# Elementwise arithmetic moved from GpSimd to VectorE in a float32 encoder of an S5 layer and a spatial-gating layer

## The chip, the core and the metric

The kernel runs on one core of a Trainium2 chip. The metric is device time in microseconds (us) of one execution, as the median of several runs. The profiled execution is a separate one, of which the hardware profiler recorded every instruction.

## The reference, cut to what matters

Two layers over 256 tokens of 2048 channels, all in float32. Each layer has a token mixer and a feed-forward part; each of these four parts ends with an RMSNorm of its sum, whose weights multiply it before it is added to the residual stream, and the next part begins with another RMSNorm.

```python
for i in range(DEPTH):                       # 2 layers
    g = norm_g[i]
    hn = rms_norm(h, g[0])
    m = s5_mixer(hn, ...) if i % 2 == 0 else sgu_mixer(hn, ...)
    h = h + rms_norm(m, g[1])
    f = squared_relu_mlp(rms_norm(h, g[2]), ffn_w_up[i], ffn_w_down[i])
    h = h + rms_norm(f, g[3])
```

`rms_norm(x, g)` is `x * rsqrt(mean(x * x) + eps) * g`. The S5 mixer ends with a gated linear unit: `z = gelu(y); z = z * sigmoid(z @ w_glu); return z @ w_out`, where `y` comes from a linear recurrence over time.

## The kernel before

The 256 tokens are two token tiles of 128 (`n` is 0 or 1). Every large product is split into three to keep float32 accuracy: a weight `w` is sent as a high half `hi` (rounded to the matrix engine's fast format, made by ScalarE in line 145) and a low half `lo = w - hi` (line 146, on the engine in `state["lo"]`), and the activations likewise; a step multiplies hi by hi, hi by lo and lo by hi (lines 166 to 172).

A **panel** is 1024 output columns; a **step** of a panel is 128 rows of weights, so twelve products of 512 columns (three products, two column halves, two token tiles). Weights come in chunks of two steps, on the DMA queue of SP, into three buffers, from the gated linear unit on four; a chunk's buffer is free, and the next chunk's load is issued, when the low half of its last step is made (lines 148 to 152). `issue_cast` (lines 133 to 152) makes high and low halves two steps ahead of the products; `state["hold"]` stops it, and `force` overrides that. There are three buffers each for high and low halves. Smaller work is put between steps with `at(delay, fn)`, which runs `fn` so many steps later. The order of the instructions on each engine is the order in which the program writes them out; nothing reorders them.

The order of work around the change:

- **The end of a part** is `Tail.run` (lines 354 to 407). Its first panel (output columns 0 to 1023) is evicted by `take`, squared for the norm's sum, and multiplied by the norm's weights on GpSimd (`scaled(G, 0, n)`, line 360). The second panel runs all but its last three steps for both token tiles; then the three steps are run for tile 0 alone (line 374), then for tile 1, half by half (lines 384 and 386). Behind tile 0's products VectorE evicts them, works out the norm's factor (`rstd`: fifteen small operations, among them line 334 and three Newton steps in lines 246 to 248) and makes the residual of block 0 of tile 0 (`resid`, line 351; a block is 512 columns).
- The next part begins with `next_panel` (lines 409 to 464): TensorE transposes block 0 of tile 0 (`tiles(0)`, line 298, which reads the residual), ScalarE and VectorE make high and low halves of it (lines 305 and 307), and TensorE runs three steps for tile 0. Meanwhile VectorE makes the factor and the residual of tile 1, and TensorE does the same for tile 1. Blocks 1 to 3 follow between later steps (`hook`). The first two low halves of weights of the next part are made on GpSimd (`state["lo"] = G` in line 389 and the forced `issue_cast` in line 390), and so are the products of the second panel with the norm's weights (line 453).
- There are three such **seams**: S5 mixer to feed-forward, feed-forward to spatial gating, and spatial gating to the second feed-forward. The fourth tail has `dst` and ends the kernel: there two residuals of tile 0 go through ScalarE and GpSimd (`resid_g`, lines 343 to 347), and the output is stored by SP (`put`).
- In the **gated linear unit's first panel** (lines 1047 to 1083) all low halves up to step 12 are made on GpSimd (lines 1047 and 1082). Between its steps stand the last part of the recurrence: `scan_some(3, 99)` in line 1066, forty operations on VectorE over the last 512 channels, written behind step 2; `y_group` on TensorE, with ScalarE's copies; and `z_t`, transposes of `z`.

## Time and profile before

| | us |
|---|---|
| median of 3 runs | 2763.17 |
| lowest and highest run | 2760.88, 2763.52 |
| span of the profiled execution | 2762.2 |
| TensorE busy in it (products) | 2678.5 |
| VectorE busy | 1598.9 |
| ScalarE busy | 1260.0 |
| GpSimd busy | 102.6 |

TensorE is busy for 97% of the span, VectorE for 58%, ScalarE for 46% and GpSimd for 4%. The granted TensorE clock is 0.979 of full speed on the mean. Times in the trace are counted from the start of the span. In a row, the numbers in front are the start and the duration in us, the name of the engine follows (PE is TensorE, DVE VectorE, ACT ScalarE, POOL GpSimd, SPq the issuing queue of SP), then the line of the kernel, the operation, the tiles written and read, their shapes and the number of instructions that the row merges. In square brackets stands how long the engine was idle just before, and what it waited for. A pair of merged rows on one engine can overlap a little, as instructions are pipelined.

### The profile page before, as it was taken

Reading aid. Unit: us, or ns where it says so; the run is one execution under the profiler, and the core shown is the slowest. Engines: PE = TensorE matmul, PEld = TensorE weight load, DVE = VectorE, ACT = ScalarE, POOL = GpSimd, SP = SyncE. Lnnn points to the kernel's source line nnn. Section 1 sums busy time; section 2 is a strip of 40 time slices with the busy share of each in tenths; the row PEclk is TensorE's granted clock in tenths of the full one; section 3 lists DMA queues with packets and bytes.
Section 4 is the critical chain, followed back from the end, with each engine's and each line's share of the span. In section 5 each row is a group of like instructions: output and inputs, shape, how many; then the busy total and the mean of one; then the engine's idle time right before and its main releaser. Section 6 shows DMA issues by size and latency. Waiting matters only on the chain.

```text
span 2762.2 us, 30556 instructions
## 1 busy us (share of the span) xinstructions
PE 2678.5 (97%) x12327; PEld 2159.4 (78%) x12327; DVE 1598.9 (58%) x1798; ACT 1260.0 (46%) x1440; POOL 102.6 (4%) x60
## 2 busy tenths in 40 slices
PE   8989998999999999989999999999989999999997
PEld 4547887888888888778887788888868888888885
DVE  6684456545555555675547745555575455555556
ACT  5455544544443444454444544444444444444443
POOL 0103101000000000110000000000010000000001
PEclk9987999999999999999999999999999999999998
DMA  7432574555555555565656555555645555555553
GB/s 185 139 107 73 173 231 164 190 190 185 193 186 196 185 188 192 183 185 197 198 191 204 184 198 183 192 189 193 220 167 186 195 188 193 184 197 184 193 187 107
DMA packets 149437, 502.29 MB, mean 182 GB/s; under 512 B 21792, under 2 KB 30128, under 8 KB 147888
## 3 DMA queue, kind: packets, MB, share of 16 engines
q1 hardware_dynamic: 148704, 500.02, 53.8%
q8 instruction: 96, 1.57, 0.2%
q10 hardware_dynamic: 592, 0.33, 0.0%
q14 instruction: 45, 0.37, 0.0%
HBM read 494.02 MB, written 6.29 MB: 181 GB/s over the span
## 4 chain that ended last, share of the span: by engine, by line
PE 90%; DVE 3%; ACT 2%; issue 2%; POOL 0%; DVEq 0%; POOLq 0%; ACTq 0%
PE acc L171 82%; PE acc L183 2%; PE tr L264 2%; PE acc L892 1%; PE tr L1237 1%; PE acc L895 1%; DVE lo L146 0%; PE acc L827 0%; DVE st L246 0%; DVE st L247 0%; DVE st L248 0%; ACT g L881 0%; DVE g L351 0%; POOL lo L146 0%; ACT hi L145 0%
## 5 line engine op out<-in xcount | busy, mean ns | idle before, releaser
L171 PE MATMUL acc<-hi,sl_g 128*128 128x512 f32 x6912 | 1886.0, 392 | 2.5 <-DVE g L321 1.1
L171 PEld LDWEIGHTS acc<-hi,sl_g 128*128 128x128 f32 x6912 | 1298.1, 189 | 276.6 <-ACT sl_g L305 2.7
L146 DVE TENSOR_TENSOR lo<-raw,hi 128x1024 fp32r<-128x1024 f32 x639 | 791.6, 1241 | 654.5 <-ACT hi L145 647.3
L171 PE MATMUL acc<-lo,sl_g 128*128 128x512 f32 x3456 | 1067.9, 390 | 3.3 <-DVE lo L146 2.6
L145 ACT ACTIVATE hi<-raw 128x1024 fp32r<-128x1024 f32 x652 | 691.0, 1061 | 797.4 <-PE acc L171 794.9
L171 PEld LDWEIGHTS acc<-lo,sl_g 128*128 128x128 f32 x3456 | 649.5, 188 | 140.6 <-DVE lo L146 3.7
L146 DVE TENSOR_TENSOR lo<-spare,hi 128x1024 fp32r<-128x1024 f32 x206 | 252.5, 1226 | 287.0 <-ACT hi L145 287.0
L145 ACT ACTIVATE hi<-spare 128x1024 fp32r<-128x1024 f32 x212 | 224.7, 1061 | 324.7 <-PE acc L171 324.7
L269 DVE TENSOR_TENSOR sl_g<-tr,sl_g 128x512 fp32r<-128x512 f32 x104 | 67.3, 687 | 115.1 <-ACT sl_g L268 115.1
L340 POOL TENSOR_TENSOR g<-g,big 128x1024 f32<-128x1024 f32 x16 | 41.9, 2631 | 2302.8 <-ACT big L329 2294.9
L183 PE MATMUL acc<-raw,g 128*128 128x512 f32 x256 | 122.6, 626 | 0.1
L268 ACT ACTIVATE sl_g<-tr 128x512 fp32r<-128x512 f32 x104 | 57.1, 595 | 87.8 <-PE tr L264 87.4
L183 PEld LDWEIGHTS acc<-raw,g 128*128 128x128 f32 x256 | 49.2, 201 | 53.4 <-issue 52.5
L1144 DVE TENSOR_TENSOR g<-acc,g 128x1024 f32<-128x1024 f32 x48 | 56.4, 1217 | 0.0
L264 PE MATMUL tr<-ident,big 128*128 128x128 f32 x416 | 55.9, 276 | 0.1
L264 PEld LDWEIGHTS tr<-ident,big 128*128 128x128 f32 x416 | 48.9, 142 | 8.4 <-ACT big L1238 1.7
L892 PE MATMUL acc<-big,g 128*64 128x64 f32 x256 | 36.2, 281 | 10.7 <-issue 6.3
L901 ACT ACTIVATE big<-acc 32x256 f32<-32x256 f32 x64 | 23.9, 374 | 40.9 <-PE acc L895 40.2
L1123 DVE TENSOR_TENSOR big<-big 128x1024 f32<-128x1024 f32 x32 | 39.2, 1226 | 5.2 <-ACT big L1122 3.0
L892 PEld LDWEIGHTS acc<-big,g 128*64 128x64 f32 x256 | 25.8, 176 | 19.7 <-issue 8.9
L1122 ACT ACTIVATE big<-acc,st 128x1024 f32<-128x1024 f32 x32 | 35.8, 1119 | 8.7 <-PE acc L171 8.7
L1238 ACT ACTIVATE big<-tr,bsT 128x384 f32<-128x384 f32 x32 | 18.6, 582 | 41.7 <-PE tr L1237 40.7
(174 smaller groups left out, 927.8 us busy)
## 6 DMA issues: line engine op xcount, KB each, us to landing
raw<-in_ffn_w_up_dram SPq DMA_DIRECT2D x96, 1024.0 KB, 5.0
raw<-in_ffn_w_down_dram SPq DMA_DIRECT2D x96, 1024.0 KB, 5.3
raw<-in_sgu_w_in_dram SPq DMA_DIRECT2D x72, 1024.0 KB, 5.0
raw<-in_sgu_w_out_dram SPq DMA_DIRECT2D x36, 1024.0 KB, 5.3
spare<-in_ffn_w_up_dram SPq DMA_DIRECT2D x32, 1024.0 KB, 5.0
spare<-in_ffn_w_down_dram SPq DMA_DIRECT2D x32, 1024.0 KB, 5.3
spare<-in_sgu_w_in_dram SPq DMA_DIRECT2D x24, 1024.0 KB, 5.1
raw<-in_s_w_in_dram SPq DMA_DIRECT2D x15, 1024.0 KB, 6.1
```

The costliest lines, as they stand in the source:

```text
L145: S.activation(out=hi, in_=src, func=AF.Copy)
L146: state["lo"].tensor_tensor(out=lo, in0=src, in1=hi.bitcast(F32), op=ALU.subtract)
L171: T.matmul(half(ps, j), lhsT=l, rhs=r[:, j * 512:(j + 1) * 512], start=first and w == 0, stop=last and w == which[-1])
L183: T.matmul(ps[n][:, j * 512:(j + 1) * 512], lhsT=lhs[n], rhs=raw_t[i][:, k, j * 512:(j + 1) * 512], start=first, stop=last)
L264: T.transpose(out=ps[:, a * 256 + n * 128:a * 256 + n * 128 + 128], in_=src(kt + a, n), identity=ident)
L268: S.activation(out=slab.hi[:, o:o + 512], in_=ps, func=AF.Copy)
L269: V.tensor_tensor(out=slab.lo[:, o:o + 512], in0=ps, in1=slab.hi32[:, o:o + 512], op=ALU.subtract)
L340: eng.tensor_tensor(out=self.m[:, n, c], in0=self.m[:, n, c], in1=self.gbc[:, c], op=ALU.mult)
L892: T.matmul(o[gp], lhsT=dst[:, q, gp, :], rhs=w2[:, 2 * r + gp, :], start=True, stop=False)
L1122: S.activation(out=tmp[n], in_=ps[n], func=AF.Relu, scale=rs[:, n:n + 1])
L1123: V.tensor_tensor(out=tmp[n], in0=tmp[n], in1=tmp[n], op=ALU.mult)
L1144: V.tensor_tensor(out=acc[:, n, c], in0=ps[n], in1=acc[:, n, c], op=ALU.add)
```

## The change

All elementwise arithmetic of GpSimd goes to VectorE, and some of it to another place in the order:

- `state["lo"]` is gone: every low half is made on VectorE, in the tails, in the gated linear unit and elsewhere.
- `scaled(0, n)` is put behind steps 2 and 4 of the tail's second panel.
- `scaled(1, 0)` stands right behind the first residual of tile 0 in `run`; `scaled(1, 1)` stands in `next_panel` behind the transposes of block 1.
- The forced casts of the next part's first two steps at the end of `run` are gone; `issue_cast(first + 3, True)` in `next_panel`, which stays, now makes all of the first three, behind the copies of `tiles(0)`.
- The last tail has its own order: tile 1's first half is run before tile 0's factor is worked out, `resid_g` is gone, and residuals are made 1024 columns at a time, each followed by its stores.

```diff
-        def scaled(self, eng, p, n):
+        def scaled(self, p, n):
             c = slice(p * 1024, (p + 1) * 1024)
-            eng.tensor_tensor(out=self.m[:, n, c], in0=self.m[:, n, c], in1=self.gbc[:, c],
-                              op=ALU.mult)
-
-        def resid_g(self, b, n):
-            c = slice(b * 512, (b + 1) * 512)
-            S.activation(out=self.m[:, n, c], in_=self.m[:, n, c], func=AF.Copy, scale=self.r[n])
-            G.tensor_tensor(out=self.h[:, n, c], in0=self.h[:, n, c], in1=self.m[:, n, c],
-                            op=ALU.add)
-
-        def resid(self, b, n):
-            c = slice(b * 512, (b + 1) * 512)
+            V.tensor_tensor(out=self.m[:, n, c], in0=self.m[:, n, c], in1=self.gbc[:, c],
+                            op=ALU.mult)
+
+        def resid(self, b, n, nb=1):
+            c = slice(b * 512, (b + nb) * 512)
             V.scalar_tensor_tensor(out=self.h[:, n, c], in0=self.m[:, n, c], scalar=self.r[n],
                                    in1=self.h[:, n, c], op0=ALU.mult, op1=ALU.add)
...
             for n in range(2):
-                self.scaled(G, 0, n)
+                at(2 + 2 * n, lambda n=n: self.scaled(0, n))
...
             if dst is not None:
-                self.scaled(G, 1, 0)
+                split_steps(*args, 1, [((0,), all3)])
+                srcs = [self.take(ps, 1, 1, 0)]
+                self.square(srcs[0], 1, 1)
+                self.rstd(0)
+                self.scaled(1, 0)
+                split_steps(*args, 1, [((1,), all3)])
+                for b in (0, 2):
+                    self.resid(b, 0, 2)
+                    put(0, b, b + 2)
+                srcs.append(self.take(ps, 1, 1, 1))
+                self.square(srcs[1], 2, 1)
+                split_done(panels[1], nk - 3, nk)
+                self.scaled(1, 1)
+                self.rstd(1)
+                for b in (0, 2):
+                    self.resid(b, 1, 2)
+                    put(1, b, b + 2)
+                return
             self.rstd(0)
-            if dst is None:
-                self.resid(0, 0)
-            else:
-                self.resid_g(2, 0)
+            self.resid(0, 0)
+            self.scaled(1, 0)
             split_steps(*args, 1, [((0,), all3)])
             srcs = [self.take(ps, 1, 1, 0)]
             split_steps(*args, 1, [((1,), all3)])
             srcs.append(self.take(ps, 1, 1, 1))
             split_done(panels[1], nk - 3, nk)
-            state["hold"], state["lo"] = False, G
-            issue_cast(panels[1][0] + nk + 2, True)
+            state["hold"] = False
...
-            state["lo"] = V
             tiles(0)
             issue_cast(first + 3, True)
             self.last()
             self.rstd(1)
             self.resid(0, 1)
-            for n in range(2):
-                self.scaled(G, 1, n)
...
             issue_cast(first + 5, True)
             trans(1)
+            self.scaled(1, 1)
             run_panel(panel, slabs, ps, 3, hook=hook)
...
         y_group(0, 2)
-        state["lo"] = G
         issue_cast(glu_p[0][0] + 2, True)
...
         z_t(1, 3)
-        state["lo"] = V
         run_panel(glu_p[0], slab_z, pg, 11, 16)
```

## Rows read from the trace of the kernel before

**Rows 1.** The chain of work that ended last: its line by engine on the page, with shares of the span, and one piece of the chain in order of time (start, us, what).

```profile
PE 90%; DVE 3%; ACT 2%; issue 2%; POOL 0%; DVEq 0%; POOLq 0%; ACTq 0%
...
914.74 84.35 PE acc L171 x372
```

**Rows 2.** TensorE's waits over the whole span, the longest in total (engine, line waited for, us in total, times, longest).

```profile
PE tr L298 <- DVE g L351: 28.2, 6, 8.4
```

**Rows 3.** GpSimd's groups of instructions by line and shape (count, busy us and mean ns, idle time before them and what ended it).

```profile
L340 POOL TENSOR_TENSOR g<-g,big 128x1024 f32<-128x1024 f32 x16 | 41.9, 2631 | 2302.8 <-ACT big L329 2294.9 <-issue 5.2 <-DVE g L325 2.7
...
L146 POOL TENSOR_TENSOR lo<-raw,hi 128x1024 fp32r<-128x1024 f32 x13 | 31.3, 2419 | 65.1 <-ACT hi L145 65.1
```

**Rows 4.** The timeline of the second seam, all engines, in order of start.

```profile
1170.22 0.16 DVE L334 SCALAR_TENSOR_TENSOR st<-st 128x1 f32<-128x1 f32 x1 [0.41 <-ACT big L329]
...
1171.90 4.64 POOL L146 TENSOR_TENSOR lo<-spare,hi 128x1024 fp32r<-128x1024 f32 x2 [14.53 <-ACT hi L145]
...
1171.95 2.30 DVE L246 TENSOR_TENSOR st<-st 128x1 f32<-128x1 f32 x1
...
1179.63 1.28 DVE L321 TENSOR_TENSOR g<-acc,g 128x512 f32<-128x512 f32 x2
...
1179.77 1.11 PE L298 MATMUL tr<-ident,g 128*128 128x128 f32 x4 [7.74 <-DVE g L351]
...
1180.49 1.15 ACT L305 ACTIVATE sl_g<-tr,gT 128x128 fp32r<-128x128 f32 x4 [7.78 <-PE tr L298]
...
1181.15 1.13 DVE L307 SCALAR_TENSOR_TENSOR sl_g<-tr,gT,sl_g 128x128 fp32r<-128x128 f32 x4 [0.24 <-ACT sl_g L305]
...
1184.21 2.21 DVE L334 SCALAR_TENSOR_TENSOR st<-st 128x1 f32<-128x1 f32 x1
...
1190.36 0.73 PE L171 MATMUL acc<-hi,sl_g 128*128 128x512 f32 x2 [0.24 <-ACT sl_g L305]
```

**Rows 5.** Two prices on VectorE: the product of two 128x1024 tiles (group by line, over the whole span), and two low halves of weights in a row (timeline, from 1236).

```profile
L1123 DVE TENSOR_TENSOR big<-big 128x1024 f32<-128x1024 f32 x32 | 39.2, 1226 | 5.2 <-ACT big L1122 3.0
...
1236.05 2.34 DVE L146 TENSOR_TENSOR lo<-raw,hi 128x1024 fp32r<-128x1024 f32 x2
```

**Rows 6.** The timeline of the first seam, VectorE, and TensorE's first product for the second token tile.

```profile
443.03 0.16 DVE L334 SCALAR_TENSOR_TENSOR st<-st 128x1 f32<-128x1 f32 x1 [0.50 <-ACT big L329]
...
457.13 0.14 DVE L253 TENSOR_TENSOR st<-st 128x1 f32<-128x1 f32 x1
...
457.58 0.16 DVE L334 SCALAR_TENSOR_TENSOR st<-st 128x1 f32<-128x1 f32 x1
...
459.98 0.75 DVE L351 SCALAR_TENSOR_TENSOR g<-g,st,g 128x512 f32<-128x512 f32 x1
...
461.68 0.73 PE L171 MATMUL acc<-hi,sl_g 128*128 128x512 f32 x2 [0.24 <-ACT sl_g L305]
```

**Rows 7.** The timeline: a wait of TensorE in the first seam's last panel, and its first transposes in the third seam.

```profile
408.94 0.74 PE L171 MATMUL acc<-lo,sl_g 128*128 128x512 f32 x2 [0.34 <-DVE lo L146]
...
2022.02 1.11 PE L298 MATMUL tr<-ident,g 128*128 128x128 f32 x4 [7.68 <-DVE g L351]
```

**Rows 8.** The timeline of the gated linear unit's first panel: the scan on VectorE (its first and last operation, one plain one of 480 elements, and the three longest), the high half of the fifth step on ScalarE, and on TensorE the sixth step's first products and the transposes behind the eighth.

```profile
241.55 1.19 DVE L856 TENSOR_TENSOR g<-g,sc_t 128x992 f32<-128x992 f32 x1 [0.63 <-ACT g L838]
...
245.96 1.06 ACT L145 ACTIVATE hi<-raw 128x1024 fp32r<-128x1024 f32 x1
...
246.20 0.66 DVE L856 TENSOR_TENSOR g<-g,sc_t 128x480 f32<-128x480 f32 x1
...
247.34 2.80 DVE L858 TENSOR_TENSOR g<-g,g 128x480 f32<-128x480 f32 x1
...
256.57 2.47 DVE L859 TENSOR_TENSOR g<-g,g 128x224 f32<-128x224 f32 x1
...
259.08 2.72 DVE L856 TENSOR_TENSOR g<-g,sc_t 128x480 f32<-128x480 f32 x1
...
265.47 0.71 PE L171 MATMUL acc<-hi,sl_g 128*128 128x512 f32 x2
...
267.09 1.19 DVE L859 TENSOR_TENSOR g<-g,g 128x992 f32<-128x992 f32 x1
...
274.75 0.60 PE L264 MATMUL tr<-ident,big 128*128 128x128 f32 x4
```

**Rows 9.** Busy time by stretch: the stretch and its length; then busy us and instructions of PE, PEld, DVE, ACT and POOL; then the granted clock, the DMA share and GB/s.

```profile
240.00:252.00 12.00, 8.22 (x65) 6.35 (x65) 11.18 (x14) 6.91 (x7) 2.54 (x1) 0.64 0.24 89
...
275.00:296.00 21.00, 20.64 (x179) 16.16 (x178) 3.26 (x5) 14.08 (x25) 6.71 (x3) 1.00 0.53 183
...
1180.00:1186.00 6.00, 5.97 (x17) 4.46 (x17) 5.28 (x10) 3.42 (x9) 1.98 (x1) 0.55 1.17 232
```

**Rows 10.** The timeline of TensorE behind its wait in the spatial gating layer.

```profile
1463.72 0.73 PE L171 MATMUL acc<-lo,sl_g 128*128 128x512 f32 x2 [2.27 <-DVE lo L146]
...
1465.21 1.00 PE L171 MATMUL acc<-lo,sl_g 128*128 128x512 f32 x2
...
1468.77 0.92 PE L171 MATMUL acc<-hi,sl_g 128*128 128x512 f32 x2
```

**Rows 11.** The timeline of the end of the kernel: VectorE's eviction of the first token tile, and SP's first stores of the last eight.

```profile
2738.95 1.29 DVE L321 TENSOR_TENSOR g<-acc,g 128x512 f32<-128x512 f32 x2 [1.76 <-PE acc L171]
...
2755.66 1.72 SPq L368 DMA_DIRECT2D out_dram<-g  x4
```

More of the change, by code (lines that the diff above doesn't have):

```diff
@@ L94 @@
     chunks, steps = [], []
-    state = {"dma": 0, "done": 0, "cast": 0, "step": 0, "ext": None, "lo": V, "hold": True}
+    state = {"dma": 0, "done": 0, "cast": 0, "step": 0, "ext": None, "hold": True}
     raw_t, hi_t, lo_t = {}, {}, {}
@@ L145, in issue_cast @@
                 S.activation(out=hi, in_=src, func=AF.Copy)
[L146 removed]
+                V.tensor_tensor(out=lo, in0=src, in1=hi.bitcast(F32), op=ALU.subtract)
                 hi_t[s], lo_t[s] = hi, lo
@@ L395, in run @@
             self.last = last
-            if dst is not None:
-                self.last()
-                for b in range(2):
-                    self.resid(b, 0)
-                self.resid_g(3, 0)
-                self.scaled(G, 1, 1)
-                self.rstd(1)
-                put(0)
-                for b in range(4):
-                    self.resid(b, 1)
-                    if b % 2:
-                        put(1, b - 1, b + 1)
         def next_panel(self, panel, slabs, gcol):
```

1 line of the change is left out of this document (removed).

## Prediction

> **What bounds the kernel now.** I read the chain that ended last first [rows 1]: TensorE carries 90% of it, so a change on other engines is worth only what it does to TensorE's waits. The list of those waits comes second [rows 2]: its largest entry is the transposes of line 298 waiting for VectorE's line 351, 28.2 us in six waits. These six are the three seams between layers, two at each: at the end of a layer TensorE has nothing to multiply until the residual of the first 512 columns is done, once for each token tile. Third, what GpSimd does [rows 3]: 16 products with the norm's weights at 2631 ns and 19 low halves at some 2.4 us, at the seams and in one other place, the gated linear unit's first panel.
>
> The timeline of the second seam shows why VectorE is late there [rows 4]. Its Newton steps are 128x1 operations. The one at 1171.95 takes 2.30 us and ends at 1174.25; GpSimd's pair of low halves starts at 1171.90 and has 2.32 us for each, so its first ends at 1174.22. The operation of line 334 has the same size and takes 0.16 us at 1170.22, with GpSimd silent, and 2.21 us at 1184.21, with GpSimd at work. The reader should see that VectorE's small operations last as long as GpSimd's large ones beside them, and that TensorE waits 7.74 us behind this.
>
> **The change at the three seams.** Removed there: two low halves and two products on GpSimd. Added to VectorE: the product `scaled(1, 0)` between the first residual and the evictions, two more low halves, and `scaled(1, 1)` after the second block's transposes. I work out VectorE's new line, in program order, for the second seam. Line 334 starts at 1170.22, as before. From line 334 to the residual takes 2.40 us where GpSimd is silent (457.58 to 459.98 [rows 6]), so the first residual starts at 1172.62. Behind it on VectorE: that residual 0.75 [rows 6], product 1.23 [rows 5], two evictions 1.28 and four low halves of transposed blocks 1.13 [rows 4], three low halves of weights at 1.17, 3.5 [rows 5], the second rstd 2.85 (457.13 to 459.98 [rows 6]): 10.74 us. So the second token tile's residual starts at 1183.36. From there to its first product takes 1.70 us (459.98 to 461.68 [rows 6]): 1185.06 against 1190.36 [rows 4], **5.3 us gained**. ScalarE does not break the line: four copies are 1.15 us [rows 4] and a high half is 1.06 [rows 8], and both run under the product and the evictions.
>
> First seam, same sum: 443.03 + 2.40 + 10.74 + 1.70 = 457.87 against 461.68 [rows 6], **3.8 us**; it is less since GpSimd's last product stretched nothing there. Third seam: its first wait is 7.68 us [rows 7] against 7.74, so 5.3 us again. Together **14.4 us**. In the first seam's last panel TensorE also waited 0.34 us for a low half that GpSimd's products had delayed [rows 7]; I take these **0.3 us**.
>
> What is late next: TensorE still waits, first about a microsecond for the first residual, then some 2 us for the first high half (ScalarE now makes all three behind the copies), then about 3 us for the second residual, because two low halves and a product stand before it. The products `scaled(0, n)` stand behind two steps of the last panel. A step is twelve products at 0.227 us (84.35 us for 372 [rows 1]), 2.7 us, and holds one low half of 1.2, so they are covered; without that cover each costs its 1.23. `scaled(1, 1)` is covered likewise, with the low halves of two steps ahead of it. The weight load that the first two casts release moves back on SP by some 3 us, and behind the loads that the next layer issues; several chunks are in flight, so I count zero, and a microsecond at each seam if they are not enough.
>
> **The gated linear unit.** Thirteen low halves go back to VectorE, whose scan of the last 512 channels ran beside GpSimd's. In program order the fifth low half stands before the scan, the sixth and seventh behind it. The fifth's high half is made at 245.96 and takes 1.06 us, ScalarE being full until then [rows 8]. VectorE began the scan at 241.55; now it first waits for 247.02 and makes the low half, 1.2 us, so the scan starts at 248.3. In return its stretched operations shrink: 2.80, 2.47 and 2.72 us where such a one takes 0.66 or less [rows 8], 6.0 us in all. Its length, 241.55 to 268.28, falls from 26.7 to 20.7; it ends at 269.0, and the sixth low half is there at 270.2. TensorE reached that step at 265.47 and will stand behind two products, some 4 us. After 270.2 it has ten products and two steps, 7.7 us, to reach 277.9, where it was at 274.75 before [rows 8]: **3.1 us lost**. The bounds are 0 and 4.2, all that the wait can be.
>
> **The clock.** From 1180 to 1186, right behind the 7.74 us wait, the granted clock is 0.55, near the lower of its two levels [rows 9]; that is in the numbers above, and goes or stays with the wait. Behind one wait of 2.27 us two products took 0.73 us at 1463.72, but 1.00 at 1465.21 and still 0.92 at 1468.77; by an estimate half of these 3.5 us, 1.7, was lost [rows 10]. The new waits, 3 us at each seam and 4 us in the linear unit, lie between these. Bounds: 0 to 1.7 at each seam; 0 to 6.8 in the linear unit (half speed over some 13.6 us, as around 250, where the clock is 0.64 [rows 9]). I take **1.0** for each seam: the 2.27 us row is the nearest, but I do not expect all three to pay it; and **2.0** in the linear unit, by the same row and a longer wait.
>
> **The end of the kernel.** The last stage is VectorE, ScalarE and GpSimd alone. New: the second token tile's first half is evicted at about 2741.7 (2738.95 [rows 11], nine products, half of 1.28), then rstd 2.85, product 1.23, two wide residuals at most 1.5 each (twice 0.75), eviction 0.64, square 1.06 at most (as a high half of twice its width [rows 8]), product 1.23, rstd 2.85, wide residual 1.5: 2756.0 at most. Before, the first of the last eight stores was issued at 2755.66 [rows 11], and SP's issue of these eight sets the end. What the stretched operations give back is paid for by the products in line. I count 0, and half a microsecond either way.
>
> **Sum:** -14.4 - 0.3 + 3.0 (clock, seams) + 3.1 + 2.0 (linear unit) = -6.6 us. The profiled span is 2762.2; the median of the runs is 2763.17, 1.0 above. From the median: **2756.6 us**.
>
> **Rivals.** (a) *The linear unit costs nothing*, because TensorE comes later to the sixth low half than before: without the 5.1 us the time is 2751.5. Against it: TensorE's waits ahead of it are on ScalarE, and stay. 0.17, with what lies between. (b) *The clock eats it*: 1.7 at each seam and 6.8 in the linear unit: -14.7 + 5.1 + 3.1 + 6.8 = 0.3, or 2763.5. For it: every long wait in the trace has a slow stretch behind it; against it: whole panel steps come behind the new ones, not sparse work. 0.25 for the space from 2757.6 to there. (c) *Slower*: the stretching is not GpSimd's doing but belongs to small operations beside ScalarE's casts. Then the first residual comes as before, and the 3.5 us of added work (product and two low halves) less the 2.1 us of line 334 stand in the line: 1.4 us later at each seam, 3.5 if line 334 stays long; with 5.1 in the linear unit 2772 to 2779. It decides as soon as one Newton step still shows over 2 us. Against it: the coinciding ends. 0.04. (d) *VectorE becomes the bound of the linear unit's panel*, with all thirteen low halves paid, 16.0 us in place of 3.1: 2769.5. For it: VectorE is busy 11.18 of 12 us from 240 to 252; against it: 3.26 of 21 from 275 to 296 [rows 9], so the work has room on either side of the scan. 0.04. The Trainium skill, page Perfetto Trace Analysis, section Optimizing Scalar/DVE Operations, gives this rule: when VectorE is saturated, moving some work to another engine, even GpSimd, may make sense. It adds that these two share a read port, so that it might not help; the trace bears the first half out for the scan alone, and the second at the seams. That the change does not do what it says I exclude, by the diff.
>
> **How the numbers follow.** The forecast, 2753.5 to 2757.6, has 0.50; (a) 0.17, (b) 0.25, (c) and (d) 0.08. A measurement of this kernel can tell about 0.2%, 5.5 us, from no change; that border is 2757.6. So faster 0.67, same 0.25, slower 0.08. The range runs from below (a) to near (b), 2750 to 2762.5; it leaves out (c), (d) and the ends.
>
> **What would show it.** No arithmetic is left on GpSimd; all 128x1 operations take near 0.16 us; line 298's waits fall from 28.2 to some 13 us; line 171 waits for line 146 near 266, about 4 us; the granted clock behind each seam's second wait shows which of the two clock cases holds. I am wrong if Newton steps stay long, if the clock falls at every seam and for long in the linear unit, or if the scan starts near 241 as before.

## The result, and the profile after

The changed kernel took 2744.64 us (median of 5 runs, 2743.36 to 2752.01), the kernel before 2760.88 us in the same comparison (5 runs, 2756.96 to 2763.52). The ratio is 0.9947, with a 95% interval of 0.9932 to 0.9963. That is 16.2 us less, where 6.6 were forecast. Three of all executions in this document, whose granted clock was 0.45 to 0.71 on the mean, took 3586 us or more and are left out of every median and range.

The first line of the page: GpSimd is left with 12.8 us, all of it memsets and set-up. VectorE is busy for no longer than before (1598.9 us then), although it does GpSimd's work as well.

```profile
PE 2670.4 (97%) x12327; PEld 2154.8 (79%) x12327; DVE 1591.8 (58%) x1831; ACT 1258.2 (46%) x1438; POOL 12.8 (0%) x23
```

TensorE's waits over the whole span (engine, line waited for, us in total, times, longest). The first entry is what [rows 2] show as 28.2 us; the other two are new or grown: TensorE now waits once for a low half in the linear unit (4.1 us), and at each seam for the first high half (2.0).

```profile
PE tr L298 <- DVE g L345: 6.7, 6, 2.0
...
PE acc L171 <- DVE lo L146: 6.3, 2, 4.1
PE acc L171 <- ACT hi L145: 5.9, 3, 2.0
```

The second seam's timeline, which answers to [rows 4]. Look at three things. No small operation is long: line 334 has 0.16 us, and so have all others. TensorE's first transposes wait 1.32 us where they waited 7.74. The second wait is 0.53 us, because the twelve products ahead of it take 5.49 us, where the same twelve take 3.09 at full clock (`scan_split`, shown further down).

```profile
1162.33 0.16 DVE L334 SCALAR_TENSOR_TENSOR st<-st 128x1 f32<-128x1 f32 x1 [0.41 <-ACT big L329]
...
1164.65 0.75 DVE L345 SCALAR_TENSOR_TENSOR g<-g,st,g 128x512 f32<-128x512 f32 x1
1165.32 1.22 DVE L340 TENSOR_TENSOR g<-g,big 128x1024 f32<-128x1024 f32 x1
1165.46 0.66 PE L298 MATMUL tr<-ident,g 128*128 128x128 f32 x4 [1.32 <-DVE g L345]
...
1168.07 5.49 PE L171 MATMUL acc<-hi,sl_g 128*128 128x512 f32 x12 [1.96 <-ACT hi L145]
...
1174.86 0.75 DVE L345 SCALAR_TENSOR_TENSOR g<-g,st,g 128x512 f32<-128x512 f32 x1
1175.67 0.66 PE L298 MATMUL tr<-ident,g 128*128 128x128 f32 x4 [0.53 <-DVE g L345]
...
1176.56 0.72 PE L171 MATMUL acc<-hi,sl_g 128*128 128x512 f32 x2 [0.24 <-ACT sl_g L305]
```

Busy time by stretch (stretch, length, busy us of PE, PEld, DVE, ACT, POOL, then the granted clock). The half clock lies ahead of 1176, between the two waits; behind the second wait it is 1.00.

```profile
1166.00:1172.00 6.00, 4.04 (x11) 3.13 (x10) 6.00 (x10) 5.24 (x11) 0.00 (x0) 0.59 0.44 67
1172.00:1176.00 4.00, 3.47 (x13) 2.44 (x12) 3.08 (x17) 0.00 (x0) 0.00 (x0) 0.77 0.78 264
1176.00:1182.00 6.00, 5.76 (x31) 4.68 (x30) 4.90 (x8) 3.84 (x8) 0.00 (x0) 1.00 0.10 11
```

The 0.55 of [rows 9] belongs to the same place in the kernel before: between its two waits, on the same twelve products. Behind its second wait, of 2.11 us, the clock was 1.00 too. Its timeline of TensorE, and the stretch behind that wait:

```profile
1180.91 5.08 PE L171 MATMUL acc<-hi,sl_g 128*128 128x512 f32 x12
...
1189.46 0.66 PE L298 MATMUL tr<-ident,g 128*128 128x128 f32 x4 [2.11 <-DVE g L351]
```

```profile
1189.40:1195.40 6.00, 5.70 (x31) 4.67 (x31) 4.51 (x9) 3.45 (x7) 0.00 (x0) 1.00 0.00 0
```

The linear unit's first panel, which answers to [rows 8]: VectorE waits for the fifth high half, makes the low half, and only then begins the scan; the operation that took 2.80 us takes 0.65; the sixth low half stands behind the whole scan, and TensorE behind it.

```profile
239.97 1.23 DVE L146 TENSOR_TENSOR lo<-raw,hi 128x1024 fp32r<-128x1024 f32 x1 [6.51 <-ACT hi L145]
241.11 1.19 DVE L850 TENSOR_TENSOR g<-g,sc_t 128x992 f32<-128x992 f32 x1
...
246.91 0.65 DVE L852 TENSOR_TENSOR g<-g,g 128x480 f32<-128x480 f32 x1
...
261.47 2.35 DVE L146 TENSOR_TENSOR lo<-raw,hi 128x1024 fp32r<-128x1024 f32 x2
...
262.74 1.22 PE L171 MATMUL acc<-lo,sl_g 128*128 128x512 f32 x2 [4.06 <-DVE lo L146]
```

**Where the time went.** Spans alone mislead here, so I cut every profiled execution at the same six points, all of them starts of TensorE's instructions: the transposes near 204 us, the third group of 128x64 products behind them (`y_group(1, 0)`), the sixth (`y_group(1, 3)`), and at each seam the first product of the second token tile; the last stretch ends with the span. In us, for all runs of this study that left a comparable profile:

| kernel | to y(1,0) | to y(1,3) | to seam 1 | to seam 2 | to seam 3 | to the end |
|---|---|---|---|---|---|---|
| before | 39.83 | 42.78 | 175.12 | 728.68 | 842.29 | 729.55 |
| before_again | 39.22 | 42.64 | 175.09 | 728.67 | 842.30 | 729.51 |
| changed | 32.85 | 47.09 | 169.97 | 722.74 | 836.49 | 728.25 |
| after_again | 32.82 | 47.19 | 169.96 | 722.75 | 836.41 | 728.22 |
| glu_only | 40.47 | 48.18 | 175.00 | 728.71 | 842.28 | 729.56 |
| glu_on_gpsimd | 32.77 | 42.44 | 169.95 | 722.75 | 834.81 | 728.72 |
| scan_split | 40.44 | 46.65 | 169.99 | 722.73 | 837.99 | 728.23 |
| gp_product | 32.87 | 47.11 | 171.87 | 724.43 | 838.25 | 728.25 |
| gp_memset | 40.51 | 48.18 | 169.88 | 722.76 | 834.89 | 729.87 |
| products_on_gpsimd | 32.87 | 47.16 | 172.58 | 726.20 | 840.04 | 729.73 |
| lows_on_gpsimd | 32.87 | 47.14 | 171.58 | 724.41 | 838.33 | 729.39 |
| glu_gp_later | 40.63 | 41.49 | 169.28 | 722.16 | 834.23 | 728.58 |
| engine_only | 32.81 | 42.41 | 169.71 | 721.63 | 835.04 | 729.74 |

Between the first profiles of before and after: -7.0, +4.3, -5.15, -5.94, -5.80 and -1.3 us, together -20.9. The first of these six is no work of the change, as the experiments show; without it the sum is -13.9.

### The profile page after: what moved, and what is told of

It reads as the page before. It is cut to its first block, busy times and chain, and to the rows that moved or that the text cites. A ratio compares the mean times of both kernels' runs of the same rounds, so it can differ in the third digit from the quotient of the medians.

```text
span 2741.3 us, 30524 instructions
## 1 busy us (share of the span) xinstructions
PE 2670.4 (97%) x12327; PEld 2154.8 (79%) x12327; DVE 1591.8 (58%) x1831; ACT 1258.2 (46%) x1438; POOL 12.8 (0%) x23
## 4 chain that ended last, share of the span: by engine, by line
PE 91%; DVE 3%; ACT 2%; issue 1%; DVEq 0%; ACTq 0%
PE acc L171 84%; PE acc L183 2%; PE tr L264 2%; PE tr L1229 1%; PE acc L886 1%; DVE lo L146 1%; ACT g L875 1%; PE acc L821 1%; PE acc L889 0%; DVE g L321 0%; DVE g L345 0%; ACT big L895 0%; ACT g L832 0%; DVE g L340 0%; ACT hi L145 0%
## 5 line engine op out<-in xcount | busy, mean ns | idle before, releaser
L146 DVE TENSOR_TENSOR lo<-spare,hi 128x1024 fp32r<-128x1024 f32 x212 | 259.6, 1225 | 287.1 <-ACT hi L145 287.1
L886 PE MATMUL acc<-big,g 128*64 128x64 f32 x256 | 32.8, 260 | 10.5 <-issue 6.4
L1230 ACT ACTIVATE big<-tr,bsT 128x384 f32<-128x384 f32 x32 | 18.6, 582 | 41.6 <-PE tr L1229 40.6
L1222 DVE TENSOR_TENSOR big<-big,g 128x768 f32<-128x768 f32 x32 | 30.7, 958 | 1.1
```

Source lines behind the costliest of these rows:

```text
L146: V.tensor_tensor(out=lo, in0=src, in1=hi.bitcast(F32), op=ALU.subtract)
L886: T.matmul(o[gp], lhsT=dst[:, q, gp, :], rhs=w2[:, 2 * r + gp, :], start=True, stop=False)
L1222: V.tensor_tensor(out=vt[:, :, c], in0=vt[:, :, c], in1=t[h % 2].unsqueeze(1).to_broadcast([128, 2, HD]), op=op)
```

## The experiments

Theory 1 was: each part has its own price, the three seams gain about 5.5 us each because GpSimd's operations that read SBUF hold VectorE's operations up, the linear unit loses 4.3, and the 7 us ahead of it come and go by themselves. Times are medians; "before" in brackets is the kernel before in the same comparison.

### Is the stretch ahead of the linear unit part of the change?

The changed kernel and the kernel before, both unaltered, once more.

> The changed kernel once more, unaltered, for a second profile and five more pairs of times. Theory 1 (7 us of the difference of the two profiles is a stretch of half clock ahead of the gated linear unit that comes and goes from execution to execution; the rest, about 14 us, is the change): the time is 2743 to 2752 again, the seams of the profile stand at the same distances from one another as in the first (722.7 us from the first to the second seam's first product of the second token tile, 836.5 from the second to the third), to within 1 us, and the stretch from 202 to 226 us may last anything from 3 to 24 us. Rival (the change itself removes the stretch): it is short again here and in every kernel that holds the changed parts, and long in every one that holds the old ones.

> The kernel before, unaltered, for a second profile and more times. Theory 1 (the stretch of half clock ahead of the linear unit comes and goes from execution to execution in both kernels): times in two groups, near 2756.5 and near 2763; the profile has 32.8 or some 40 us from the transposes at 204 to the third y_group, and whichever it is, the seams stand 728.7 and 842.3 us apart as in the first profile, to within 2 us, and the time from the third to the sixth y_group is 42.8. Rival (the stretch belongs to the kernel before): all times near 2763 and the profile as the first.

The changed kernel took 2748.95 us (2743.36 to 2752.03; before 2762.19), ratio 0.9952 (0.9939 to 0.9965); the kernel before 2762.95 (2756.06 to 2764.41), ratio 1.0 (0.999 to 1.0009). The distances from seam to seam are within 0.1 us of the first profiles in both. For the first stretch, compare busy time from 200 to 226 us (the granted clock is the third number from the end) in four executions. First the second profile of the kernel before, then that of the changed one:

```profile
200.00:226.00 26.00, 21.85 (x150) 16.80 (x150) 0.85 (x2) 13.60 (x27) 6.46 (x3) 0.61 0.33 94
```

```profile
200.00:226.00 26.00, 21.71 (x183) 16.03 (x182) 7.20 (x8) 18.73 (x34) 1.81 (x1) 0.93 0.41 124
```

That looks like an effect of the change, and is not one: two kernels below whose seams are the changed kernel's (scan_split and gp_memset; neither is altered ahead of the linear unit's scan) have it too.

```profile
200.00:226.00 26.00, 22.11 (x148) 17.12 (x149) 3.36 (x4) 13.44 (x27) 1.67 (x1) 0.57 0.41 123
```

```profile
200.00:226.00 26.00, 21.84 (x148) 16.74 (x148) 3.88 (x4) 13.41 (x27) 1.81 (x1) 0.59 0.40 122
```

The column "to y(1,0)" has two values over thirteen profiles, 32.8 and 39 to 40.6, and they don't follow the code: engine_only is the kernel before word for word up to the first seam and has 32.8, glu_gp_later has the changed kernel's seams and 40.6. The times fall into two groups as well. Of all 71 times of the kernel before, 20 lie from 2755.6 to 2759.1 (mean 2757.2) and 51 from 2760.6 to 2765.5 (mean 2763.2); of the changed kernel's ten, five lie from 2743.4 to 2745.7 (mean 2744.1) and five from 2748.9 to 2752.0 (mean 2750.7). Group against group the change is worth 13.1 and 12.5 us. The 16.2 us of the first comparison hold, beside that, some 3 us of luck: three of its five changed runs fell in the lower group, and two of its five of before. That the groups of times are the two clock stretches was seen where there is a profile (2743.36 and 2745.69 have the short one, 2763.29 the long one); that it holds for the others is inferred, and no profile of the kernel before caught its lower group.

### What the linear unit costs

The changed kernel with this part undone (in `glu_only` the other way round: the kernel before with this part alone).

```diff
-                V.tensor_tensor(out=lo, in0=src, in1=hi.bitcast(F32), op=ALU.subtract)
+                state["lo"].tensor_tensor(out=lo, in0=src, in1=hi.bitcast(F32), op=ALU.subtract)
...
+        state["lo"] = G
         issue_cast(glu_p[0][0] + 2, True)
...
+        state["lo"] = V
         run_panel(glu_p[0], slab_z, pg, 11, 16)
```

> The changed kernel, with the low halves of the gated linear unit's first panel made on GpSimd again and all else as changed. Theory 1 (each part of the change has its own price: the three seams gain about 5.5 us each, the end some 1 us, the linear unit loses): the wait of TensorE for the sixth low half, 4.06 us in the changed kernel, is gone, the panel's stretched scan operations of 2.5 to 2.8 us are back, and from the last y_group to the end of the panel the kernel is 4.3 us shorter than the changed one: about 2740.3 against 2744.6 us. Rival (the linear unit's panel is better off for the change too, by the 6.9 us by which it starts earlier): it starts some 7 us later again, as in the kernel before, and the time is 2744.6 plus 7 less 4, about 2747. The instructions up to 200 us are the same in both kernels, so by theory 1 the stretch of half clock from 202 to 226 us, which was there in the profile of before and almost absent in that of after, comes and goes from execution to execution.

> The kernel before, with only the low halves of the gated linear unit's first panel moved to VectorE; seams and end as before. Theory 1: this part alone costs 4.3 us from the last y_group to the end of the panel, by the difference of the two traces, with a wait of about 4 us for the sixth low half: about 2765 against 2760.9 us, seams unchanged (six waits of line 298, some 28 us, Newton steps of 2.2 to 2.3 us still there at the seams). The prediction's sum was 5.1, about 2766. Rival (this part brings the 7 us by which the changed kernel's panel began earlier): about 2758. The stretch of half clock from 202 to 226 us may be there or not; the two milestones before and behind it tell it from the panel's own cost.

Undone: 2744.56 us (2738.65 to 2746.35; before 2762.19), ratio 0.9935 (0.9921 to 0.9948); the stretch from y(1,0) to y(1,3) falls from 47.09 to 42.44, and the seams stay. Alone: 2769.08 (2762.68 to 2769.69), ratio 1.0027 (1.0017 to 1.0036); that stretch rises from 42.78 to 48.18. The wait ends 26.0 us behind the start of y(1,0) in the changed kernel and in `glu_only`, when VectorE has the low half ready; TensorE stands there for 4.06 us in the one and 4.80 in the other, as it comes later or earlier, and behind the longer wait the half clock costs 1.1 us more. The pairs are not alike in clock: between profiles that are (y(1,0) to y(1,1) within 0.2 us) the part costs 4.65 us (changed against glu_on_gpsimd) and 6.7 (gp_memset against glu_gp_later). The times say some 5 to 6, each group against its like: 5.0 and 5.3 undone, 5.5 and 5.8 alone. Theory 1 holds, with its 4.3 too low: the part is a loss by itself and is paid for by the seams. In the kernel with the part undone the scan is stretched again, as the timeline of GpSimd and VectorE shows (2.81 us for 0.65), but no instruction of TensorE waits for it there:

```profile
242.45 2.55 POOL L146 TENSOR_TENSOR lo<-raw,hi 128x1024 fp32r<-128x1024 f32 x1 [7.89 <-ACT hi L145]
```

```profile
242.71 2.81 DVE L852 TENSOR_TENSOR g<-g,g 128x480 f32<-128x480 f32 x1
```

Is the loss the order, or VectorE's load? The scan in four pieces, with low halves between them:

```diff
-        scan_some(3, 99)
+        scan_some(3, 5)
...
-        run_panel(glu_p[0], slab_z, pg, 3, 5)
+        run_panel(glu_p[0], slab_z, pg, 3, 4)
+        scan_some(3, 2)
+        run_panel(glu_p[0], slab_z, pg, 4, 5)
+        scan_some(3, 2)
...
-        run_panel(glu_p[0], slab_z, pg, 5, 8)
+        run_panel(glu_p[0], slab_z, pg, 5, 7)
+        scan_some(3, 99)
+        run_panel(glu_p[0], slab_z, pg, 7, 8)
```

> The changed kernel, with the scan of the last 512 channels cut into four pieces that stand behind steps 2, 3, 4 and 6 of the linear unit's panel, so that the low halves of steps 5 to 7 stand between them on VectorE. Theory 1 (the 4.06 us wait for the sixth low half is an order effect: VectorE has room, but the low half stands behind the whole scan): that wait falls under 1 us and the time falls by 2 to 4 us against the changed kernel, about 2742. Rival (VectorE is the bound of this panel): the scan then ends later by the low halves that are put before it, TensorE waits for the scan's states at y_group in place of the low half, and the time is within 1 us of the changed kernel's, about 2744.6.

2751.62 us (2744.2 to 2751.74), ratio 0.9958 (0.9946 to 0.9971); in the table 46.65, against 48.18 for gp_memset, which has the same long stretch ahead. TensorE's waits from 240 to 300 us in this kernel have no entry for a low half; instead the changed kernel's one wait for line 875 (3.8 us, ahead of the scan) has become two, and the new one is for the scan's last states:

```profile
PE acc L886 <- ACT g L875: 5.7, 2, 3.8
PE acc L886 <- DVE g L873: 0.4, 1, 0.4
```

So theory 1 fails here: its wait is gone, but only 1.5 us come back. The rival's wait, for the scan's states, has come in its place, 2.3 us in all, and the y_group behind it runs at half clock (8.6 us, from 278.06 to 286.69, where y(1,1) took 5.1). Whether VectorE's load alone bounds this panel isn't settled. In the changed kernel VectorE has no idle time from the fifth low half to the eighth (239.97 to 265.56); in this order it has some ahead of the scan's last four operations, so another order might do better:

```profile
267.97 0.69 DVE L269 TENSOR_TENSOR sl_g<-tr,sl_g 128x512 fp32r<-128x512 f32 x1 [1.71 <-ACT sl_g L268]
```

### Does GpSimd hold VectorE up, and by what?

The changed kernel, with one operation of GpSimd's put back at each seam that nothing waits for: a product (reads two tiles of SBUF), or three memsets (read nothing). In both a copy of eight columns stands ahead, which only places them in time.

```diff
+            if dst is None:
+                G.tensor_copy(g7[:, 3072:3080], self.m[:, 0, 2040:2048])
+                G.tensor_tensor(out=g7[:, 3072:4096], in0=self.m[:, 0, 0:1024],
+                                in1=self.gbc[:, 0:1024], op=ALU.mult)
             self.rstd(0)
```

> The changed kernel, with one added operation on GpSimd at each of the three seams just ahead of the first token tile's norm factor: a product of two 128x1024 tiles in SBUF, written to a scratch area that nothing reads (and a copy of eight columns that places it in time). Nothing on VectorE, ScalarE or TensorE waits for it. Theory 1 (GpSimd's operations that read SBUF hold up VectorE's operations of two inputs until they end): one small operation of the factor, near 0.16 us in the changed kernel, shows about 2.2 us or what is left of GpSimd's product when it begins, the first residual comes some 2 us later and so do TensorE's first transposes: about +2 us at each seam, +6 in all, near 2750.5. Rival (the small operations were long for another reason, the order or ScalarE's casts beside them): they stay near 0.16 us and the time stays at 2744.6.

> The changed kernel, with three memsets of 128x1024 on GpSimd into the scratch area at the same place of each seam, in place of the product of the run beside it: GpSimd is busy, but reads nothing. Theory 1 with a conflict of reads: VectorE's small operations stay near 0.16 us and the time at 2744.6. Rival (whatever GpSimd does in SBUF holds VectorE up, writes too): they show up to 2 us and the time rises by up to 6 us.

With the product 2756.02 us (2749.7 to 2757.32; before 2762.99), ratio 0.997 (0.9958 to 0.9982); with the memsets 2751.2 (2744.5 to 2752.2), ratio 0.9953 (0.9937 to 0.997). The table has +1.9, +1.7 and +1.8 us at the seams for the product; for the memsets nothing at the first two. (The stretch to seam 3 also holds TensorE's wait of 2.3 us in the spatial gating layer. From that wait's end to seam 3 kernels with equal seams took 563.0 us where half clock followed the wait and 561.4 where none did; the memset kernel is one of the latter, so its -1.6 is not the memsets'; nor is its +1.6 to the end, which is half clock behind its third seam's second wait.) The second seam with the product: line 334 begins 0.55 us behind the product's start and ends at 1168.63, with the product's end at 1168.60.

```profile
1166.21 2.39 POOL L392 TENSOR_TENSOR big<-g,big 128x1024 f32<-128x1024 f32 x1
1166.76 1.87 DVE L334 SCALAR_TENSOR_TENSOR st<-st 128x1 f32<-128x1 f32 x1 [0.41 <-ACT big L329]
```

The same place with the memsets, which last longer: line 334 and the Newton step under them take 0.16.

```profile
1170.74 2.98 POOL L393 MEMSET big<- 128x1024 f32 x3
1171.31 0.16 DVE L334 SCALAR_TENSOR_TENSOR st<-st 128x1 f32<-128x1 f32 x1 [0.41 <-ACT big L329]
1171.88 0.16 DVE L246 TENSOR_TENSOR st<-st 128x1 f32<-128x1 f32 x1
```

Theory 1 holds, and rival (c) of the prediction falls: in these runs a small operation with two inputs in SBUF waits for GpSimd's product, which reads SBUF, to its end, and not for a memset, which only writes. The Trainium skill, page SBUF — State Buffer, section Who interferes with whom, gives this rule: VectorE's instructions with two SBUF inputs contend with a GpSimd instruction that reads SBUF, and not with one that only writes. These two runs agree with both halves of it, 1.87 us against 0.16.

### Which of the two kinds did the harm, and does the order matter?

First all products with the norm's weights (those of the last tail too), then the first two low halves of each seam, on GpSimd at the changed kernel's places in the program (for the second, `state["lo"]` is put back as above):

```diff
-            V.tensor_tensor(out=self.m[:, n, c], in0=self.m[:, n, c], in1=self.gbc[:, c],
+            G.tensor_tensor(out=self.m[:, n, c], in0=self.m[:, n, c], in1=self.gbc[:, c],
```

```diff
             tiles(0)
+            state["lo"] = G
+            issue_cast(first + 2, True)
+            state["lo"] = V
             issue_cast(first + 3, True)
```

> The changed kernel, with the products with the norm's weights made on GpSimd, each at the place in the order where the changed kernel has it; the low halves stay on VectorE. Theory 1: the product behind the first residual runs some 2.6 us on GpSimd beside VectorE's evictions, which read the accumulator and one tile of SBUF, and holds them up, so that the second token tile's first product comes 1 to 3 us later at each seam than in the changed kernel: +3 to +9 us, about 2750. Rival (the gain at the seams is from the low halves alone, and VectorE's line is shorter by the products' 1.23 us): 1 us earlier at each seam, about 2742.

> The changed kernel, with the first two low halves of weights behind each seam made on GpSimd, at the changed kernel's place in the order (behind the first transposes); products stay on VectorE. Theory 1: GpSimd makes them in some 2.4 us each beside the factor of the second token tile, of which one or two small operations are held up by up to 2.3 us, while VectorE's line is shorter by 2.3: 0 to +2 us at each seam, 2744.6 to 2751. Rival (the products were the harm and the low halves harmless on GpSimd): VectorE's line is shorter and nothing is held up, -1 to -2 us at each seam, down to 2739.

Products: 2763.75 us (2753.72 to 2765.19), ratio 0.9997 (0.9984 to 1.0011), in the table +2.6, +3.5 and +3.6 us at the seams and +1.5 to the end. That is 11.2 in all, above the 3 to 9 expected; the median shows 19, as six of the ten runs fell in the upper group. Low halves: 2750.25 (2747.98 to 2750.81), ratio 0.9954 (0.9939 to 0.9969), +1.6, +1.7 and +1.8. Neither kind was harmless. Theory 1 holds for the low halves. For the products its harm came, but not its way: the evictions take 1.28 us as in the changed kernel. The product that the program writes behind the first residual needs nothing of that residual, and GpSimd, which has its own order, begins it as soon as ScalarE's square is done, ahead of the residual; there it holds up a Newton step of the first factor until its end (1168.3), and the next product does the same to line 253 of the second factor (2.33 us):

```profile
1165.93 2.38 POOL L340 TENSOR_TENSOR g<-g,big 128x1024 f32<-128x1024 f32 x1 [12.92 <-ACT big L329]
1166.45 1.87 DVE L246 TENSOR_TENSOR st<-st 128x1 f32<-128x1 f32 x1
```

The second seam with the low halves on GpSimd: the two take 5.71 us there, VectorE's line 253 takes 2.33 us instead of 0.15 and ends with them, and the second residual comes 11.84 us behind the first, against 10.21, although VectorE does two operations fewer.

```profile
1164.84 0.75 DVE L345 SCALAR_TENSOR_TENSOR g<-g,st,g 128x512 f32<-128x512 f32 x1
...
1168.34 5.71 POOL L146 TENSOR_TENSOR lo<-spare,hi 128x1024 fp32r<-128x1024 f32 x2 [718.78 <-ACT hi L145]
...
1171.74 2.33 DVE L253 TENSOR_TENSOR st<-st 128x1 f32<-128x1 f32 x1
...
1176.68 0.75 DVE L345 SCALAR_TENSOR_TENSOR g<-g,st,g 128x512 f32<-128x512 f32 x1
```

Then the engine without the order: the kernel before, with GpSimd's work at the three seams on VectorE at the old places.

```diff
-                self.scaled(G, 0, n)
+                self.scaled(V if dst is None else G, 0, n)
...
-            state["hold"], state["lo"] = False, G
+            state["hold"] = False
...
-                self.scaled(G, 1, n)
+                self.scaled(V, 1, n)
```

> The kernel before, with the products with the norm's weights and the first two low halves of each of the three seams on VectorE at the very places in the order where the kernel before has them; the linear unit's low halves and the last tail stay as they were, on GpSimd. It differs from the kernel with the linear unit on GpSimd again (about 2739 or 2745) by the order at the seams and by the end. Theory 1 (the engine is the cause, not the order): all small operations at the seams take near 0.16 us, the line from first to second residual holds two low halves but no product, 9.2 to 10.3 us, and each seam gains 5 to 7 us against the kernel before, 15 to 20 in all: 2739 to 2742 where the stretch ahead of the linear unit is short, 6 more where it is long. Rival (the order is the cause): the two low halves, now ahead of the first transposed blocks' low halves on VectorE, hold TensorE's first products up by 2.3 us, and the products ahead of the later blocks do so again by up to 2.4; each seam gains 0 to 2.5 us, 2749 to 2757 (short), 2755 to 2763 (long).

2737.91 us (2736.32 to 2746.86; before 2762.18), ratio 0.9926 (0.9909 to 0.9943): the lowest median of this study, with four of its six runs in the lower group. Its seams are 5.4, 7.05 and 7.25 us shorter than before, the third with the 1.6 us in it by which the half clock behind the spatial gating layer's wait is missing here. Compared with glu_on_gpsimd, which has the changed order, they differ by -0.2, -1.1 and +0.2. So the gain at the seams is the engine's, and the new order adds nothing to it. What the old order costs is seen in its second seam: TensorE waits 2.10 us for the copies of the first transposed blocks, behind the two low halves; but the second residual comes 9.07 us behind the first, as no product stands between.

```profile
1160.45 0.75 DVE L351 SCALAR_TENSOR_TENSOR g<-g,st,g 128x512 f32<-128x512 f32 x1
...
1162.31 2.35 DVE L146 TENSOR_TENSOR lo<-spare,hi 128x1024 fp32r<-128x1024 f32 x2
...
1164.98 3.94 PE L171 MATMUL acc<-hi,sl_g 128*128 128x512 f32 x10 [2.10 <-DVE sl_g L307]
...
1169.52 0.75 DVE L351 SCALAR_TENSOR_TENSOR g<-g,st,g 128x512 f32<-128x512 f32 x1
```

### What is late next at a seam

The product behind the first residual put behind the second one, alone and together with the linear unit's low halves on GpSimd:

```diff
             self.resid(0, 0)
-            self.scaled(1, 0)
...
             self.resid(0, 1)
+            self.scaled(1, 0)
```

> The changed kernel with the product behind the first residual of each seam put behind the second token tile's residual, and nothing else. Theory 1: first product of the second token tile 0.5 to 1.1 us earlier after each first residual than in the changed kernel (10.2 to 10.3 us from first transposes to second transposes there), 1.5 to 3.3 us in all, about 2742 where the stretch ahead of the linear unit is short. Rival: a new wait takes it back, 2743.4 as in the changed kernel.

> Two edits of the changed kernel together: the low halves of the gated linear unit's first panel on GpSimd again (that edit alone measured 4.65 us shorter than the changed kernel between the y_groups of the panel), and at each seam the product behind the first residual put behind the second token tile's residual, which takes its 1.13 us out of VectorE's line from residual to residual. Theory 1 (the second wait of TensorE at a seam ends with VectorE's line): in an execution in which TensorE waits over 1.1 us for the second residual, that residual and the second token tile's first product come 1.1 us earlier; where half clock already fills most of the wait (0.5 to 1.0 us left in the changed kernel) only what is left of it, 0.5 to 1.0. So 4.65 + 1.5 to 3.4 us below the changed kernel: 2736 to 2738.5 in executions in which the stretch of half clock ahead of the panel is short, some 7 us more where it is long. Rival (the product is then late for the evictions of a later block, or pushes the low halves that stand behind it): a new wait of line 171 for a low half, or of line 298, of about 1 us at each seam, and nothing gained over the edit of the linear unit alone, 2739 (short) to 2746 (long).

Alone: 2747.14 us (five runs, 2742.39 to 2749.07), ratio 0.9946 (0.9932 to 0.996), which can't be told from the changed kernel; its profiled execution is one of the three left out, so the table has no row for it. Together: 2742.16 (2741.46 to 2745.58; before 2763.53), ratio 0.9935 (0.9922 to 0.9947), in an execution with the long stretch ahead of the linear unit. The seams gain 0.7, 0.6 and 0.6 us over glu_on_gpsimd, and not 1.1: once the product is away, VectorE has 0.33 us without work, for the high half, which is most of what is missing. Without the first stretch this is the shortest kernel of the table: its other five columns add up to 2495.7 us, against 2498.5 for engine_only and 2498.7 for glu_on_gpsimd; that the median of engine_only is lower comes from the first stretch.

```profile
2002.37 1.13 DVE L307 SCALAR_TENSOR_TENSOR sl_g<-tr,gT,sl_g 128x128 fp32r<-128x128 f32 x4
2003.83 2.36 DVE L146 TENSOR_TENSOR lo<-spare,hi 128x1024 fp32r<-128x1024 f32 x2 [0.33 <-ACT hi L145]
```

## Why the prediction was right or wrong

**The mechanism was right.** GpSimd's reading operations stretched VectorE's small ones, TensorE waited behind that, and the change trades it for a loss in the linear unit. The size was not: like against like 12.5 to 13.1 us, against 6.6. By the profiles, without the first stretch, it is 13.9; of the 7.3 us between, 3.0 are the clock at the seams, 2.2 the rest of the seams, 1.3 the end and 0.8 the linear unit.

**The step that failed is the clock at the seams**, "I take 1.0 for each seam". I charged half clock behind the second wait; in the changed kernel it comes in front of it, on the twelve products with high halves, and what those lose is taken out of the wait that follows. The kernel before shows it already (its lines stand above): half clock on these products, and 1.00 behind the second wait of 2.11 us, where rival (b) has a slow stretch behind every long wait. Three executions with the same code at the second seam show it: TensorE's row of these twelve products, and its second transposes. The changed kernel's rows stand above (5.49 us; wait 0.53; 10.21 us from first to second transposes). In glu_on_gpsimd:

```profile
1163.17 0.66 PE L298 MATMUL tr<-ident,g 128*128 128x128 f32 x4 [1.32 <-DVE g L345]
1165.78 4.60 PE L171 MATMUL acc<-hi,sl_g 128*128 128x512 f32 x12 [1.96 <-ACT hi L145]
...
1173.37 0.66 PE L298 MATMUL tr<-ident,g 128*128 128x128 f32 x4 [1.63 <-DVE g L345]
```

And in scan_split:

```profile
1172.38 0.66 PE L298 MATMUL tr<-ident,g 128*128 128x128 f32 x4 [1.32 <-DVE g L345]
1174.99 3.09 PE L171 MATMUL acc<-hi,sl_g 128*128 128x512 f32 x12 [1.96 <-ACT hi L145]
...
1182.59 0.66 PE L298 MATMUL tr<-ident,g 128*128 128x128 f32 x4 [2.70 <-DVE g L345]
...
1185.35 1.79 PE L171 MATMUL acc<-hi,sl_g 128*128 128x512 f32 x4
```

The products take 5.49, 4.60 or 3.09 us, the wait behind them is 0.53, 1.63 or 2.70, and the distance is 10.21, 10.20 and 10.21: VectorE's line sets it, whatever the clock. The forecast itself had TensorE wait about 3 us there; time lost to the clock ahead of such a wait costs nothing until the wait is used up. The last row of scan_split is the other case, the one I had charged: no half clock ahead, the whole wait of 2.7 us, and half clock behind it (1.79 us for four products that take 1.07 at full clock). From the second token tile's first product to the next transposes of line 264 took 4.2 us at 13 of the 15 seams with the changed kernel's code (the runs changed, after_again, glu_on_gpsimd, scan_split and gp_memset), and 5.8 at the other two, this one and gp_memset's third, both behind a wait of 2.7. So the size, 1.6 us, was near the 1.7 of [rows 10]; what was wrong is where the half clock falls, and so how often it is paid: 3.2 us in 15 seams, 0.2 each in place of 1.0, and none in either profile of the changed kernel.

**The seams' line on VectorE.** Its gain, 5.3 us at the second seam, measured 5.9. The line from residual to residual was 10.21 us for 10.74, the way from line 334 to the first residual 2.32 for 2.40; I had added up durations of rows that overlap with the next (the product's row of 1.22 us is followed by the eviction's 1.13 us after its start). From the second residual to the first product it is 1.70, as forecast. At the first seam 5.15 for 3.8 and the 0.3 of its last panel: the line 10.30, and line 334 comes 0.8 us earlier relative to y(1,3), of which the wait of [rows 7] is 0.34; for the rest I found no row. The three seams give 16.9 us in place of 11.7 after the clock.

**What is late next** was right in kind: 1.3 to 2.0 us for the first residual, 1.96 for the first high half. Line 298's waits are 6.7 us, not some 13, since the half clock fills most of the second wait.

**The linear unit** was right in each step, and its sum of 5.1 nearly: the low half ahead of the scan, the scan's start, its end without stretched operations, a wait of "some 4 us" (4.06), 1.6 us of half clock behind it for the 2.0, and 4.3 us lost between the first profiles, some 5 to 6 by the times. Rival (a) falls with that, and rival (b), which had put 6.8 us of clock here, with the seams' clock above. So does rival (d): one wait of 4 us, not 16. Its cause may still be right for the stretch up to the scan's end, where VectorE is never idle in the changed kernel; scan_split leaves that open. The Trainium skill, page Perfetto Trace Analysis, section Optimizing Scalar/DVE Operations, holds that moving work off a saturated VectorE may make sense, to GpSimd too, but might not help as the two share a read port. Here the first half decides: GpSimd's low halves beside the scan are worth 4.65 us in glu_on_gpsimd, stretched scan and all.

**The end** I counted as 0; it is 1.3 us shorter. VectorE's last operation begins 10.5 us behind TensorE's last product, where it was 11.6, and the product kept on GpSimd brings the 11.6 back. My line of 2756.0 "at most" was near: by its distance from TensorE's last product it would end at 2755.6 on the forecast's scale. What I set it against was wrong: the first of the last eight stores (2755.66), and not the end of VectorE's last residuals, which was at 2757.0 before. In both kernels the span ends 5.2 to 5.3 us behind that end.

**The rest of the 16.2 us**, some 3, is luck as far as these runs tell: which of them had the long half-clock stretch. The forecast started from 2763.17, in the upper group; there the changed kernel takes 2750.7 us, still inside the range from 2750, and the median of 2744.64 lies in the lower group. Why an execution has the long or the short stretch stays open, and so does whether the change alters their share (in the lower group are 20 of 71 times before and 5 of 10 after).

## What to carry to other kernels

An operation that GpSimd does off the path is not free where it reads SBUF: look for VectorE's operations that last as long as GpSimd's beside them, and move those that stand beside a chain of small operations. The same move loses where VectorE has no time left and nothing waits for the operations that GpSimd stretches, so price each place by itself; here keeping the linear unit's low halves on GpSimd and moving only the seams' work is 4.4 us shorter than moving all (engine_only against the changed kernel, without the first stretch and the 1.6 us of half clock behind the spatial gating layer's wait). Before charging a slower clock, look whether a wait for another engine follows: time lost ahead of it is hidden until the wait is gone.

## What the runs showed that I had not expected

With the same code up to there, the granted clock from 200 to 226 us was 0.93 in some executions and 0.54 to 0.61 in others, which moved all behind it by 7 us; that is over half of what the change is worth. Single executions of this kernel can therefore be compared only stretch by stretch. Behind a wait of some 2 to 3 us half clock came in some executions and not in others of the same code, and cost some 1.6 us each time that it came: behind the spatial gating layer's wait in three of the five profiles with equal seams, behind the seams' second wait in two of 15. The length of the wait does not tell: in lows_on_gpsimd it came behind second waits of 2.18 and 2.13 us and not behind one of 2.27, and in products_on_gpsimd behind neither 2.60 nor 2.79.
